# Two heads' value products issued in one block, in the two column halves of the TensorE array

## The chip, the cores and the metric

The kernel runs on one core of one Trainium2 chip. The metric is the device time of one execution in microseconds (us); less is better. Stages of the program are named by the engine that a profile names: PE is TensorE's matmul, PEld its weight load, DVE is VectorE, ACT is ScalarE, POOL is GpSimd, SP is the engine whose queue issues most of the DMAs.

## The reference

One decoder layer on 512 tokens of width 1024: a norm, one wide projection, two attentions side by side, their merge through sigmoid gates, an output projection, and then a mixture of 64 experts of which each token takes two. The two attentions end in a product of probabilities and values; these products are what the change touches.

```python
# forgetting attention, 8 heads of 64, blocks of 128 queries
s = einsum('bqhd,bkhd->bhqk', qb, k) * scale + cb[..., None] - c_k[:, :, None, :]
p = softmax(where(causal, s, -inf))
o_f = einsum('bhqk,bkhd->bqhd', p, v)
# sliding window of 128 with a sink, 8 query heads over 2 key/value heads
s = einsum('bnqhgd,bnkhd->bnhgqk', qb, kw) * HEAD_DIM ** -0.5
p = softmax(concatenate([where(valid, s, -inf), sink]))[..., :-1]
o_s = einsum('bnhgqk,bnkhd->bnqhgd', p, vw)
# experts, per block of tokens
y = (silu(xb @ w1[e]) * (xb @ w3[e])) @ w2[e]
```

Everything is in float32. The weights of the 64 experts are some 400 MB, and every expert is read.

## The kernel before, in words

The program has three stretches. In the first, up to about 62 us, the inputs are normed and transposed and the first projections are made. In the second, up to about 420 us, TensorE makes the remaining projections, both attentions, the gates, the output projection and the routing. In the third the experts run, while SP's queue loads their weights in pieces of 1 MB (tiles `w`) into a ring of 16 buffers, from which they are released by TensorE's matmuls.

The attentions stand in the second stretch, in an order that is written out by hand: a manual schedule on all five engines, so each engine does its work in the order in which the code calls it. `pipeline` runs over steps i. In step i it calls `scores(i)` (TensorE, then a maximum on DVE and an exponential on ACT), `softmax(i - 1)` (DVE scales the probabilities), a piece of the projections by `take`, `probs_t(i - 2)` (TensorE transposes the probabilities; ACT or DVE copies them to `probs_T`), another piece by `take`, and `values(i - 3)`. The projections that `take` feeds in (`acc_vf`, `acc_qf`, `acc_kf`, `acc_g`) are independent of the attention at hand; they are there to keep TensorE occupied.

The sliding-window attention has 16 steps: a block t of 128 queries, a key/value head g, and a pair hp of query heads. Its values are the product of `vs` (64 columns of the key/value head g, the stationary operand) with `probs_T[i]` (256 columns: two heads), over one block of keys for t = 0 and two for the others. The result of g = 0 lies in partitions 0 to 63 of the bank `os_ps`, that of g = 1 in partitions 64 to 127. The forgetting attention has two pipelines of 16 steps: two pairs of heads, j, then four blocks of queries, qb, then the two heads x of the pair. Its values are the product of 64 columns of `vf` with 128 columns of `fprobs_T[i]`, over qb + 1 blocks of keys, into partitions 0 to 63 of `of_ps` for x = 0 and 64 to 127 for x = 1. All of these matmuls use the 128 rows of the array and 64 of its 128 columns; operands in plain float32 are run in two passes, so the profile has two records for each. The other matmuls around them use all 128 columns.

The experts' matmuls use 32 of the 128 columns, four experts in turn (`h`, L1391; `y_ps`, L1410). In the forgetting attention the steps already alternate between the two halves, but each step's values are issued by themselves, a step apart. In the sliding window two steps of the same g come one behind the other.

Lines that matter: L568 and L719 issue the values, L523 and L685 begin the scores, L545 and L698 scale probabilities, L553 and L705 transpose them, L557, L559, L708 and L710 copy them out of PSUM, and L299 to L301 are the three products of a projection in split precision.

Of the kernel before, what the change touches and what calls it, by code (L numbers as in the profile page):

```python
# [20 lines left out]
P = 128  # L21
# [4 lines left out]
HD = 64  # L26
# [71 lines left out]
def kernel(ctx: ExitStack, tc: tile.TileContext, a: dict, out: bass.AP, dbg=None):  # L98
# [3 lines left out]
    v, act, pe, gp = nc.vector, nc.scalar, nc.tensor, nc.gpsimd  # L102
# [13 lines left out]
    def acc_tile(name):  # L116
        return ps.tile([P, 512], F32, tag="acc", name=name, bufs=2)

    def s_tile(name):
        return ps.tile([P, 512], F32, tag="s", name=name, bufs=2)  # L120
# [4 lines left out]
    def o_tile(name):  # L125
        return ps.tile([P, 512], F32, tag="o", name=name, bufs=2)
# [16 lines left out]
    for name in ORDER:  # L143
        kind, i = name.rstrip("0123456789"), int(name[-1]) if name[-1].isdigit() else 0
# [31 lines left out]
    def defer(n, f):  # L176

        deferred.append([n, f])
# [214 lines left out]
    vs = main.tile([P, NT, P], F32, name="vs")  # L393
# [17 lines left out]
    for t in range(NT):  # L411
        s = slice(t * P, (t + 1) * P)
        o = acc_tile(f"acc_kv_{t}")[:, :UNIT]
# [28 lines left out]
    def att_tile(name, dt=F32):  # L442
        return att.tile([P, 512], dt, tag="u", name=name)
# [67 lines left out]
    osT_lo = blk.tile([P, 4, T], F32R, name="osT_lo", tag="ol", bufs=1)  # L511
    probs, probs_T, os_ps = {}, {}, {}

    def swa_scores(i):

        t, g, hp = i // 4, i // 2 % 2, i % 2
        k0, nk = max(t - 1, 0) * P, 256 if t else 128
        s_ps = s_tile(f"ss_ps{i}")
        s3 = s_ps.rearrange("p (h k) -> p h k", h=2)
        for j in range(2):  # L520
            h = 2 * hp + j
            lt = qsT[t, g][:, h * P:(h + 1) * P]
            pe.matmul(s3[:, j], lt, ksT[0][g][:, k0:k0 + 256], start=True, stop=False, skip_group_check=True)  # L523
            pe.matmul(s3[:, j], lt, ksT[1][g][:, k0:k0 + 256], start=False, stop=False, skip_group_check=True)
            pe.matmul(s3[:, j, 0:nk], ident_b, band if t else causal, start=False, stop=True, skip_group_check=True)
        s3 = s3[:, :, 0:nk]
        h0 = 4 * g + 2 * hp
        sm = small[:, i % 4]
        nm, e, sums = (sm[:, 2 * x:2 * x + 2] for x in range(3))
        v.tensor_reduce(nm, s3, axis=AX.X, op=OP.max, negate=True)  # L530
        v.tensor_tensor(nm, nm, neg_sinks[:, h0:h0 + 2], op=OP.min)
        v.tensor_tensor(e, sinks[:, h0:h0 + 2], nm, op=OP.add)
        p_sb = att_tile(f"sp{i}")
        p3 = probs[i] = p_sb.rearrange("p (h k) -> p h k", h=2)[:, :, 0:nk]
        for j in range(2):
            act.activation(p3[:, j], s3[:, j], AF.Exp, bias=nm[:, j:j + 1], accum_out=sums[:, j:j + 1])
        act.activation(e, e, AF.Exp)
# [21 lines left out]
            v.tensor_copy(pT[:, :n], pst[:, :n])  # L559

    def swa_values(i):
        t, g, hp = i // 4, i // 2 % 2, i % 2
        nb = 2 if t else 1
        if i % 4 == 0:
            os_ps[t] = o_tile(f"os_ps{t}")
        o = os_ps[t][g * HD:(g + 1) * HD, hp * 256:hp * 256 + 256]
        for b in range(nb):
            pe.matmul(o, vs[:, max(t - 1, 0) + b, g * HD:(g + 1) * HD], probs_T[i][:, b * 256:b * 256 + 256],  # L568
                      start=b == 0, stop=b == nb - 1, skip_group_check=True)
        if i % 4 == 3:  # L570
            s = slice(t * P, (t + 1) * P)
            o4 = os_ps[t].rearrange("p (r n) -> p r n", r=4)
            act.activation(osT_hi[:, :, s], o4, AF.Copy)
            defer(2, lambda: v.tensor_tensor(osT_lo[:, :, s], o4, osT_hi[:, :, s].bitcast(F32), op=OP.subtract))


    vf = main.tile([P, NT, T], F32, name="vf")
# [64 lines left out]
    fq, fk, fprobs, fsums, fprobs_T, of_ps, ofT = {}, {}, {}, {}, {}, {}, []  # L642
# [30 lines left out]
    def fox_at(i):  # L673

        return i // 16, i // 8 % 2, i // 2 % 4, i % 2
# [34 lines left out]
            v.tensor_copy(pT[:, :nk], pst[:, :nk])  # L710

    def fox_values(i):
        n, j, qb, x = fox_at(i)
        h = 4 * n + 2 * j + x
        qs_ = slice(qb * P, (qb + 1) * P)
        if i % 8 == 0:
            of_ps[n, j] = o_tile(f"of_ps{n}{j}")
        for b in range(qb + 1):
            pe.matmul(of_ps[n, j][x * HD:(x + 1) * HD, qs_], vf[:, b, h * HD:(h + 1) * HD],  # L719
                      fprobs_T[i][:, b * P:(b + 1) * P], start=b == 0, stop=b == qb, skip_group_check=True)  # L720
        if i % 8 == 7:
            hi = blk.tile([P, T], F32R, tag="b", name=f"ofT_hi{n}{j}")
            lo = blk.tile([P, T], F32R, tag="b", name=f"ofT_lo{n}{j}")
            act.activation(hi, of_ps[n, j], AF.Copy)
            defer(2, lambda: v.tensor_tensor(lo, of_ps[n, j], hi.bitcast(F32), op=OP.subtract))
            ofT.append((hi, lo))
# [47 lines left out]
    def swa_extra(i):  # L774
# [5 lines left out]
        if t < NT and j >= 2:  # L780
            queries_T(t, j - 2)

    pipeline(0, 16, swa_scores, swa_softmax, swa_probs_T, swa_values, QUANTA[0], swa_extra)
    take(GAP[1])
    pipeline(0, 16, fox_scores, fox_softmax, fox_probs_T, fox_values, QUANTA[1])
    take(GAP[2])
    last_exp = pipeline(16, 16, fox_scores, fox_softmax, fox_probs_T, fox_values, QUANTA[2])

    fox_done.append(True)
# [127 lines left out]
    for n in range(4):  # L917
# [5 lines left out]
        for m, src_hi, src_lo in (("pf", lambda k: ofT[k][0], lambda k: ofT[k][1]),  # L923
                                  ("ps", lambda k: osT_hi[:, k], lambda k: osT_lo[:, k])):
            hi, lo = halves_of[f"{m}{n}"]
            for j in range(2):
                b = 2 * n + j
                o = acc_tile(f"{m}_ps{b}")
# [4 lines left out]
                g = gates[b if m == "pf" else b + 8]  # L933
# [202 lines left out]
    for t in range(NT):  # L1136
        o = acc_tile(f"out_ps3_{t}")[:, :256]
# [244 lines left out]
    for b in range(N_BATCH):  # L1382
# [3 lines left out]
        for k in range(2):  # L1386
            for o, m in ((h1, "w1"), (h3, "w3")):
                for c in range(4):
                    for e in range(4):
                        s = slice(32 * e, 32 * e + 32)  # L1390
                        pe.matmul(o[s], hsel[:, 4 * k + c, s], wt[b, m, k, e][c], start=(k, c) == (0, 0),  # L1391
                                  stop=(k, c) == (1, 3), skip_group_check=True)
# [13 lines left out]
        for c in range(4):  # L1406
            for k in range(2):
                for e in range(4):
                    s = slice(32 * e, 32 * e + 32)
                    pe.matmul(y_ps[k][s], gT[:, c, s], wt[b, "w2", c // 2, e][c % 2][:, 512 * k:512 * k + 512],  # L1410
                              start=c == 0, stop=c == 3, skip_group_check=True)
# [34 lines left out]
```

## Time and profile before

| what | value |
|---|---|
| median of 3 runs | 1360.95 us (1360.67 to 1361.66) |
| the profiled execution | 1361.19 us |
| its span, first to last instruction | 1359.4 us |
| PE busy | 1215.0 us, 89% of the span |
| DVE, ACT, POOL busy | 469.3, 244.8, 96.8 us |
| records of values, sliding window (L568) | 56 |
| records of values, forgetting attention (L719) | 160 |
| DMA share, 420 us to the end | 0.99, at 410 GB/s |

The profiled execution is 0.24 us from the median, and 1.8 us of it lie outside the span. The page gives busy time per engine, a picture of the span in 40 slices, and the chain of work that ended last, followed back from the last instruction. [...]

### The profile page before, as it was taken

How to read it: one execution, taken by the hardware profiler on the slowest of the kernel's cores; microseconds unless marked ns; L12 is line 12 of the kernel's file. 1: busy time of each engine (PE TensorE's matmuls, PEld its weight loads, DVE VectorE, ACT ScalarE, POOL GpSimd, SP SyncE). 2: the span in 40 equal slices, each digit the busy share in tenths (PEclk: the TensorE clock that was granted, in tenths of full speed). 3: DMA queues.
4: the chain of work that ended last, by engine and by line, in shares of the span. 5: the costliest groups of instructions: out<-in, count | busy, mean ns of one | idle time of the engine just before them, and what ended most of it. 6: DMA issues, size and time to landing. Idle time of an engine off the chain costs nothing.

```text
span 1359.4 us, 17321 instructions
## 1 busy us (share of the span) xinstructions
PE 1215.0 (89%) x6958; PEld 637.7 (47%) x6958; DVE 469.3 (35%) x1173; ACT 244.8 (18%) x560; POOL 96.8 (7%) x135
## 2 busy tenths in 40 slices
PE   7999999999999998989798897979888798979964
PEld 7986677788996433324142333424233232423212
DVE  6776555326446343222123032212213122221203
ACT  4654343433452000000000000000000000000003
POOL 3701000003100000000000000000000000000002
PEclk8999999999999999999899899999899998999988
DMA  5311322238589999999999999999999999999994
GB/s 172 94 52 48 89 49 76 63 93 258 204 301 362 419 421 420 420 420 421 421 420 420 421 421 420 421 421 420 421 420 420 420 421 420 421 420 421 420 413 159
DMA packets 91964, 439.91 MB, mean 324 GB/s; under 512 B 9437, under 2 KB 39177, under 8 KB 43881
## 3 DMA queue, kind: packets, MB, share of 16 engines
q1 hardware_dynamic: 90152, 435.78, 80.1%
q0 software_dynamic: 1728, 2.98, 1.0%
q8 instruction: 56, 0.92, 0.3%
q14 instruction: 28, 0.22, 0.0%
HBM read 434.52 MB, written 2.10 MB: 321 GB/s over the span
## 4 chain that ended last, share of the span: by engine, by line
DMA 65%; PE 29%; DVE 3%; issue 1%; POOL 1%; ACT 1%; SPq 0%; POOLq 0%; ACTq 0%
DMA w<-in_w_dram 65%; PE acc_g L299 2%; PE acc_g L300 2%; PE acc_g L301 2%; PE of_ps L719 2%; PE h L1391 1%; PE os_ps L568 1%; PE acc_wo L301 1%; PE acc_wo L299 1%; PE acc_wo L300 1%; PE acc_kf L299 1%; PE fpT_ps L705 1%; PE acc_qf L299 1%; PE acc_qs L301 1%; PE acc_qs L299 1%
## 5 line engine op out<-in xcount | busy, mean ns | idle before, releaser
L1391 PE MATMUL h<-w,u_hi 128*32 128x512 f32 x2016 | 331.7, 629 | 63.6 <-DMA w<-in_w_dram 63.6
L1410 PE MATMUL y_ps<-w,u_hi 128*32 128x512 f32 x952 | 206.0, 605 | 33.0 <-DMA w<-in_w_dram 29.2
L1391 PEld LDWEIGHTS h<-w,u_hi 128*32 128x32 f32 x2016 | 79.8, 114 | 268.4 <-issue 128.0
L1108 PEld LDWEIGHTS g_ps<-u_hi,xc 128*128 128x128 f32 x1024 | 119.1, 191 | 49.2 <-issue 37.9
L1108 PE MATMUL g_ps<-u_hi,xc 128*128 128x128 f32 x1024 | 130.6, 281 | 1.9 <-DVE u_hi L1062 1.9
L1410 PEld LDWEIGHTS y_ps<-w,u_hi 128*32 128x32 f32 x952 | 49.1, 109 | 177.3 <-issue 87.9
L1214 DVE TENSOR_TENSOR u_lo<-c_ps,u_lo 128x512 f32<-128x512 f32 x84 | 58.1, 691 | 199.1 <-PE c_ps L1208 199.1
L1208 PE MATMUL c_ps<-xb,xb 128*128 128x512 f32 x240 | 116.7, 617 | 1.0 <-DVE u_lo L1211 0.8
L1197 DVE TENSOR_TENSOR u_hi<-h,xb 128x512 f32<-128x512 f32 x16 | 16.5, 1032 | 229.5 <-PE h L1391 229.5
L1196 ACT ACTIVATE xb<-h 128x512 f32<-128x512 f32 x16 | 9.6, 597 | 455.1 <-PE h L1391 455.1
L1189 POOL TENSOR_TENSOR xb<-xb,u_hi 128x512 f32<-128x512 f32 x16 | 20.3, 1271 | 805.9 <-DVE xb L1188 805.9
L1208 PEld LDWEIGHTS c_ps<-xb,xb 128*128 128x128 f32 x240 | 37.8, 188 | 80.0 <-DVE u_lo L1214 36.8
L1058 DVE TENSOR_SCALAR u_hi<-codes,locs,cst 128x128 f32<-128x128 f32 x60 | 20.6, 346 | 155.5 <-PE g_ps L1108 155.3
L1205 ACT ACTIVATE xb<-y_ps 128x512 f32<-128x512 f32 x30 | 17.9, 597 | 224.6 <-PE y_ps L1410 224.6
L299 PE MATMUL acc_g<-hT_hi,hi_g 128*128 128x512 f32 x128 | 54.4, 425 | 0.0
L300 PE MATMUL acc_g<-hT_lo,hi_g 128*128 128x512 f32 x128 | 50.5, 395 | 0.0
L301 PE MATMUL acc_g<-hT_hi,lo_g 128*128 128x512 f32 x128 | 50.5, 394 | 0.0
L1111 DVE TENSOR_TENSOR u_hi<-g_ps,cst 128x512 f32<-128x512 f32 x32 | 21.8, 681 | 59.9 <-PE h L1391 59.5
L1202 ACT ACTIVATE u_hi<-t_ps 128x512 f32<-128x512 f32 x16 | 9.6, 597 | 174.4 <-PE t_ps L1201 174.4
L188 DVE TENSOR_TENSOR lo_g<-raw_g,hi_g 128x1024 fp32r<-128x1024 f32 x16 | 19.6, 1226 | 36.1 <-ACT hi_g L185 36.1
L299 PE MATMUL acc_wo<-hi_wo,mT 128*128 128x256 f32 x96 | 28.6, 298 | 0.0
L301 PE MATMUL acc_wo<-hi_wo,mT 128*128 128x256 f32 x96 | 27.1, 282 | 0.1
(383 smaller groups left out, 1687.9 us busy)
## 6 DMA issues: line engine op xcount, KB each, us to landing
w<-in_w_dram SPq DMA_DIRECT2D x377, 1024.0 KB, 19.8
raw_g<-in_w_in_dram SPq DMA_DIRECT2D x16, 512.0 KB, 3.6
raw_wo<-in_w_out_dram SPq DMA_DIRECT2D x8, 512.0 KB, 4.6
x_sb<-in_x_dram SPq DMA_DIRECT2D x4, 512.0 KB, 6.3
raw_qs<-in_w_in_dram SPq DMA_DIRECT2D x4, 512.0 KB, 6.9
raw_vf<-in_w_in_dram SPq DMA_DIRECT2D x4, 512.0 KB, 4.9
raw_qf<-in_w_in_dram SPq DMA_DIRECT2D x4, 512.0 KB, 3.8
raw_kf<-in_w_in_dram SPq DMA_DIRECT2D x4, 512.0 KB, 3.8
```

What stands on the lines that cost most here:

```text
L299: pe.matmul(o, l_hi, r_hi, start=first, stop=False, skip_group_check=True)
L300: pe.matmul(o, l_hi, r_lo, start=False, stop=False, skip_group_check=True)
L301: pe.matmul(o, l_lo, r_hi, start=False, stop=last, skip_group_check=True)
L719: pe.matmul(of_ps[n, j][x * HD:(x + 1) * HD, qs_], vf[:, b, h * HD:(h + 1) * HD], fprobs_T[i][:, b * P:(b + 1) * P], start=b == 0, stop=b ...
L1058: v.tensor_scalar(sel1[:, t], labels, loc[:, 0, t:t + 1], r, op0=OP.is_equal, op1=OP.mult)
L1108: pe.matmul(g_ps[k][:, c * P:(c + 1) * P], xc[t][:, 4 * k + c], sel1[:, t], start=(t, c) == (0, 0), stop=t == NT - 1, skip_group_check=True)
L1111: v.tensor_tensor(hsel[:, 4 * k:4 * k + 4], g_ps[k].rearrange("p (c n) -> p c n", c=4), g_ffn[:, 4 * k:4 * k + 4, None].to_broadcast([P, 4 ...
L1189: gp.tensor_tensor(wsel, wsel, wtmp, op=OP.add)
L1208: pe.matmul(c_ps, w_t[:, t], ys[k], start=True, stop=True)
L1214: v.tensor_tensor(d, c_ps, d, op=OP.add)
L1391: pe.matmul(o[s], hsel[:, 4 * k + c, s], wt[b, m, k, e][c], start=(k, c) == (0, 0), stop=(k, c) == (1, 3), skip_group_check=True)
L1410: pe.matmul(y_ps[k][s], gT[:, c, s], wt[b, "w2", c // 2, e][c % 2][:, 512 * k:512 * k + 512], start=c == 0, stop=c == 3, skip_group_check= ...
```

## The change

In both attentions the values of a step with an even number are left out, and the step with the odd number behind it issues both: for each block of keys the lower half's matmul, then the upper half's. For that the two steps have to be the two halves of one bank. In the forgetting attention they are already (x = 0 and 1). In the sliding window the order of steps is turned: `swa_at` makes g the fastest index and hp the next, where hp was the fastest before. The bank is opened in the odd step. Nothing else is different: the same matmuls, the same sizes, the same steps of `take`, and on DVE, ACT, POOL and SP the same instructions in the same order.

```diff
+    def swa_at(i):
+
+        return i // 4, i % 2, i // 2 % 2
+
     def swa_scores(i):
 
-        t, g, hp = i // 4, i // 2 % 2, i % 2
+        t, g, hp = swa_at(i)
...
     def swa_values(i):
-        t, g, hp = i // 4, i // 2 % 2, i % 2
+
+        if i % 2 == 0:
+            return
+        t, _, hp = swa_at(i)
         nb = 2 if t else 1
-        if i % 4 == 0:
+        if i % 4 == 1:
             os_ps[t] = o_tile(f"os_ps{t}")
-        o = os_ps[t][g * HD:(g + 1) * HD, hp * 256:hp * 256 + 256]
         for b in range(nb):
-            pe.matmul(o, vs[:, max(t - 1, 0) + b, g * HD:(g + 1) * HD], probs_T[i][:, b * 256:b * 256 + 256],
-                      start=b == 0, stop=b == nb - 1, skip_group_check=True)
+            for g in range(2):
+                o = os_ps[t][g * HD:(g + 1) * HD, hp * 256:hp * 256 + 256]
+                pe.matmul(o, vs[:, max(t - 1, 0) + b, g * HD:(g + 1) * HD],
+                          probs_T[i - 1 + g][:, b * 256:b * 256 + 256],
+                          start=b == 0, stop=b == nb - 1, skip_group_check=True)
...
     def fox_values(i):
-        n, j, qb, x = fox_at(i)
-        h = 4 * n + 2 * j + x
+
+        if i % 2 == 0:
+            return
+        n, j, qb, _ = fox_at(i)
         qs_ = slice(qb * P, (qb + 1) * P)
-        if i % 8 == 0:
+        if i % 8 == 1:
             of_ps[n, j] = o_tile(f"of_ps{n}{j}")
         for b in range(qb + 1):
-            pe.matmul(of_ps[n, j][x * HD:(x + 1) * HD, qs_], vf[:, b, h * HD:(h + 1) * HD],
-                      fprobs_T[i][:, b * P:(b + 1) * P], start=b == 0, stop=b == qb, skip_group_check=True)
+            for x in range(2):
+                h = 4 * n + 2 * j + x
+                pe.matmul(of_ps[n, j][x * HD:(x + 1) * HD, qs_], vf[:, b, h * HD:(h + 1) * HD],
+                          fprobs_T[i - 1 + x][:, b * P:(b + 1) * P], start=b == 0, stop=b == qb,
+                          skip_group_check=True)
```

The order of PE's instructions in the sliding window, before, at the end of the pipeline step that issues the values of step 4 (`spT4`) and begins the scores of step 8 (`ss_ps8`); the last name of each row is the stationary or moving operand, and the size is that of the output:

```order
L299 MATMUL acc_vf1_1_1180<-hi_vf1_1_954,hT_hi_116 128x256
L300 MATMUL acc_vf1_1_1180<-lo_vf1_1_955,hT_hi_116 128x256
L301 MATMUL acc_vf1_1_1180<-hi_vf1_1_954,hT_lo_117 128x256
L568 MATMUL os_ps1_1274<-spT4_1198,vs_127 64x256 x2
L523 MATMUL ss_ps8_1277<-ksT00_444,qsT2_0_1206 128x256
```

The same place after, and one pipeline step further on:

```order
L299 MATMUL acc_vf1_1_1179<-hi_vf1_1_954,hT_hi_116 128x256
L300 MATMUL acc_vf1_1_1179<-lo_vf1_1_955,hT_hi_116 128x256
L301 MATMUL acc_vf1_1_1179<-hi_vf1_1_954,hT_lo_117 128x256
L527 MATMUL ss_ps8_1274<-ksT00_444,qsT2_0_1205 128x256
L528 MATMUL ss_ps8_1274<-ksT10_446,qsT2_0_1205 128x256
```

```order
L299 MATMUL acc_qf0_0_1320<-hT_hi_116,hi_qf0_0_1035 128x512
L300 MATMUL acc_qf0_0_1320<-hT_lo_117,hi_qf0_0_1035 128x512
L301 MATMUL acc_qf0_0_1320<-hT_hi_116,lo_qf0_0_1036 128x512
L576 MATMUL os_ps1_1326<-spT4_1197,vs_127 64x256
L576 MATMUL os_ps1_1326<-spT5_1258,vs_127 64x256
L576 MATMUL os_ps1_1326<-spT4_1197,vs_127 64x256
L576 MATMUL os_ps1_1326<-spT5_1258,vs_127 64x256
L527 MATMUL ss_ps9_1331<-ksT01_445,qsT2_1_1266 128x256
```

The block of step 4 is gone from its place, and its two matmuls stand between those of step 5, a pipeline step later.

PE in the forgetting attention, before, at the values of step 3 (`fpT3`; those of step 2 stand by themselves one pipeline step ahead of this):

```order
L299 MATMUL acc_qf1_0_1880<-hT_hi_116,hi_qf1_0_1717 128x512
L300 MATMUL acc_qf1_0_1880<-hT_lo_117,hi_qf1_0_1717 128x512
L301 MATMUL acc_qf1_0_1880<-hT_hi_116,lo_qf1_0_1718 128x512
L719 MATMUL of_ps00_1829<-fpT3_1878,vf_454 64x128 x2
L685 LDWEIGHTS lq_108
L685 MATMUL sf_ps7_1912<-c3_109,lq_108 128x512
```

And after:

```order
L301 MATMUL acc_qf1_0_1880<-hT_hi_116,lo_qf1_0_1718 128x512
L732 MATMUL of_ps00_1851<-fpT2_1846,vf_454 64x128
L732 MATMUL of_ps00_1851<-fpT3_1878,vf_454 64x128
L732 MATMUL of_ps00_1851<-fpT2_1846,vf_454 64x128
L732 MATMUL of_ps00_1851<-fpT3_1878,vf_454 64x128
L694 LDWEIGHTS lq_108
L694 MATMUL sf_ps7_1912<-c3_109,lq_108 128x512
```

Each pair of value blocks on PE has become one block of twice as many matmuls, in which the two halves alternate.

## Rows read from the trace of the kernel before

**Rows 1.** The page's chain that ended last, shares of the span by engine.

```profile
DMA 65%; PE 29%; DVE 3%; issue 1%; POOL 1%; ACT 1%; SPq 0%; POOLq 0%; ACTq 0%
```

**Rows 2.** That chain in order of time: start, length in us, what.

```profile
442.83 3.69 PE y_ps L1410 x32
...
447.31 16.71 DMA w<-in_w_dram
...
1266.23 19.87 DMA w<-in_w_dram
1286.17 21.37 DMA w<-in_w_dram
```

**Rows 3.** Busy time by stretch: us, engines with (records), PE clock, DMA share, GB/s.

```profile
76.00:142.00 66.00, 66.00 (x380) 48.52 (x379) 44.08 (x124) 34.19 (x99) 3.90 (x7) 1.00 0.23 61
...
153.00:206.00 53.00, 53.00 (x290) 37.69 (x289) 29.37 (x62) 22.45 (x49) 3.29 (x7) 1.00 0.24 63
```

**Rows 4.** Instructions of lines 568 and 719: ns min/median/max, first and last start.

```profile
L568 PE MATMUL os_ps<-spT,vs x56: 379/379/430, 76.3 to 141.1; 128*64 128x256 f32 x56
...
L719 PEld LDWEIGHTS of_ps<-fpT,vf x160: 132/137/137, 153.5 to 258.2; 128*64 128x64 f32 x160
L719 PE MATMUL of_ps<-fpT,vf x160: 272/273/324, 153.5 to 258.3; 128*64 128x128 f32 x160
```

**Rows 5.** PE in order of time, forgetting attention: start, length in us, what.

```profile
149.22 0.40 PE L301 MATMUL acc_g<-hT_hi,lo_g 128*128 128x512 f32 x1
149.46 0.29 PE L685 MATMUL sf_ps<-c,lq 128*128 128x256 bf16 x1
...
171.86 1.09 PE L719 MATMUL of_ps<-fpT,vf 128*64 128x128 f32 x8
172.88 0.28 PE L685 MATMUL sf_ps<-c,lq 128*128 128x256 bf16 x1
...
215.20 0.39 PE L301 MATMUL acc_g<-hT_hi,lo_g 128*128 128x512 f32 x1
215.52 0.43 PE L719 MATMUL of_ps<-fpT,vf 128*64 128x128 f32 x2
215.88 0.34 PE L685 MATMUL sf_ps<-c,lq 128*128 128x384 bf16 x1
```

**Rows 6.** PE in order of time, sliding window.

```profile
76.31 0.65 PE L568 MATMUL os_ps<-spT,vs 128*64 128x256 f32 x2
76.89 0.39 PE L523 MATMUL ss_ps<-ksT,qsT 128*128 128x256 f32 x1
...
120.69 1.08 PE L568 MATMUL os_ps<-spT,vs 128*64 128x256 f32 x4
121.70 0.38 PE L523 MATMUL ss_ps<-ksT,qsT 128*128 128x256 f32 x1
```

**Rows 7.** PE in order of time in the experts: one and three column groups of 32.

```profile
464.74 1.04 PE L1391 MATMUL h<-w,u_hi 128*32 128x512 f32 x2
465.71 0.49 PE L1108 MATMUL g_ps<-u_hi,xc 128*128 128x128 f32 x2
...
505.32 1.06 PE L1391 MATMUL h<-w,u_hi 128*32 128x512 f32 x6
506.31 0.49 PE L1108 MATMUL g_ps<-u_hi,xc 128*128 128x128 f32 x2
```

**Rows 8.** Weight loads of the same three column groups.

```profile
505.31 0.15 PEld L1391 LDWEIGHTS h<-w,u_hi 128*32 128x32 f32 x6
```

**Rows 9.** Where a producer is least ahead of PE: forgetting attention, then sliding window.

```profile
189.50 0.49 DVE L698 TENSOR_SCALAR fp<-fp,sm 128x512 f32<-128x512 f32 x1
...
191.54 0.27 PE L705 MATMUL fpT_ps<-ident,fp 128*128 128x128 f32 x1
...
77.65 0.39 ACT L557 ACTIVATE spT<-spT_ps 128x256 f32<-128x256 f32 x1
...
79.14 0.38 PE L553 MATMUL spT_ps<-ident,sp 128*128 128x128 f32 x2
```

## The prediction

> **What bounds the kernel now.** I read the chain that ended last first. By engine DMA has 65% of it and PE 29% [rows 1]. In order of time it goes over from one to the other once: at 446.5 us PE's first `y_ps` matmuls set buffers free, and from 447.3 us it runs through the weight loads, some 19.9 us each, to the experts' end [rows 2]. So the loads set the length of the third stretch, but their start hangs on PE: whatever PE saves ahead of 442 us moves every later piece forward by the same amount. Nothing in the loads has to be done faster for that; the same bytes are loaded, later pieces are only begun earlier.
>
> [...] Since busy time counts overlapping records, I take costs from distances between starts.
>
> **What one block of values costs.** There are 56 records in the sliding window and 160 in the forgetting attention, two passes for each matmul [rows 4]. In the trace they form 16 and 32 blocks.
>
> Forgetting attention [rows 5]: without values the last projection matmul is followed by the scores after 149.46 - 149.22 = 0.24 us. With a block of two records between them, entry takes 215.52 - 215.20 = 0.32 us and the block 215.88 - 215.52 = 0.36 us to the scores' start: 0.68 us, which is 0.44 us more than without. A block of eight takes 172.88 - 171.86 = 1.02 us, so each record beyond the second costs (1.02 - 0.36) / 6 = 0.11 us. Blocks of two, four, six and eight records therefore cost 0.44, 0.66, 0.88 and 1.10 us, each with a fixed part of 0.44 - 2 x 0.11 = 0.22 us for going into the half-width matmuls and out again.
>
> Sliding window [rows 6]: a block of two takes 76.89 - 76.31 = 0.58 us to the scores, one of four 121.70 - 120.69 = 1.01 us, 0.215 us for each record more. With the same 0.08 us at the entry they cost 0.66 and 1.09 us, fixed part 0.23 us.
>
> **What the change removes.** Of each two blocks of equal size one goes from its place, and its records are put between those of the other. If the two halves of the array work side by side, the block that is left costs what it costs now, and the other block's whole cost is gone.
>
> - sliding window: 2 blocks of two records (t = 0) and 6 of four: 2 x 0.66 + 6 x 1.09 = 7.9 us
> - forgetting attention: 4 pairs of heads, one block of each size: 4 x (0.44 + 0.66 + 0.88 + 1.10) = 12.3 us
> - together 20.2 us
>
> Do halves work side by side? No row of this trace has two 64-column matmuls in different halves next to each other. The nearest are the experts' 32-column groups, which have the same 128 rows, float32 and two passes. One group, two records, takes 465.71 - 464.74 = 0.97 us to the next matmul; three groups, six records, take 506.31 - 505.32 = 0.99 us [rows 7]. The second and third group cost 0.02 us together. So the lower bound of the cost of the added records is nothing, and the upper one that of running in turn, 0.11 or 0.215 us for each record. I take nothing, since the experts' rows differ in the width of the group alone.
>
> The weight loads need a look, because a step of 0.11 us is shorter than one load of 0.137 us [rows 4], and now each step has two. Alone they are already overlapped, at one for each 0.11 us. The six loads of the experts' three groups take 0.15 us in all, though one such load lasts about as long [rows 8]: loads to different columns overlap. I cost the loads at nothing; without that cover the forgetting attention's steps would double and its part of the gain would shrink to the fixed 16 x 0.22 = 3.5 us.
>
> **What the change adds or moves.** No instruction is added on any engine. DVE, ACT, POOL and SP have the same instructions in the same order, so nothing is moved past anything on a queue. Three things follow on PE.
>
> First, the earlier step's probabilities wait one pipeline step longer. Their copy is made earlier than it is needed; the cost is only that a buffer is held longer, and the order of all other work stays.
>
> Second, PE now comes sooner to the transposes and the scores in the steps that have lost their block, and may find a producer late. I looked for the smallest distance between a producer's end and PE's use with a removed block in between. In the forgetting attention DVE has scaled a step's probabilities at 189.99 us and PE transposes them at 191.54 us: 1.55 us ahead, and the removed block of six records there is worth 0.88 us. In the sliding window ACT's copy out of the transposes' bank ends at 78.04 us and PE writes that bank again at 79.14 us: 1.10 us ahead, against a removed block of 0.66 us [rows 9]. So at the tightest places 0.4 to 0.7 us are left, and I put new waits at zero. As a load, DVE's 44.08 us would stand in 66 - 7.9 = 58.1 us, 76%, which is not a bound.
>
> Third, the turned order of the sliding window wants the second g's queries one step sooner. Their transposes and copies are made in the last two steps ahead of the block, a step or more before use, and a step is over 3 us; nothing.
>
> What is late next is nothing new: PE itself, which stays full in these stretches.
>
> **The sum.** The profiled execution took 1361.19 us, of which 1359.4 us are the span; the median is 1360.95 us, and the 0.24 us between them are no matter here. 1360.95 - 20.2 = 1340.7 us, 1.5% less. Five loads of the chain take some 21.4 us in place of 19.9 us, the last of them at 1286 us [rows 2]; with the whole stretch moved by 20 us one more or one less may fall into it, 1.5 us either way.
>
> **The rivals.**
>
> *One pass too many.* The program gives each matmul's two passes one behind the other, lower half first. If starts keep to that order, the upper half's first pass can only begin with the lower half's second, and a merged block takes one step more: 8 x 0.215 + 16 x 0.11 = 3.5 us back, 1344.2 us. Against it: with three groups, six records in such an order would need four steps where one group needs two, and they take 0.99 us against 0.97 us [rows 7]. [...]
>
> *Halves in turn.* If 64-column matmuls, unlike 32-column ones, do not overlap, only the fixed parts go: 8 x 0.23 + 16 x 0.22 = 5.4 us, 1355.6 us. If only their weight loads don't, in the forgetting attention alone: 7.9 + 3.5 = 11.4 us, 1349.6 us. For it: no such pair in the trace. Against it: the experts.
>
> *A producer becomes the limit.* Each of the 24 thinned steps waits for DVE or ACT. With 0.4 us for each, about what is left at the tightest place, 9.6 us come back: 1350.4 us. Against it: both engines have idle time there [rows 3], and the places shown are the tightest.
>
> *Slower: every change of halves is a change of mode.* Into and out of a block of values cost 0.22 us together [rows 5]. If going from the lower to the upper half cost the same and nothing overlapped, a merged block of m matmuls for each head would have 2m - 1 such changes: 20 in the sliding window and 64 in the forgetting attention, 84 x 0.22 = 18.5 us against the 5.4 us of fixed parts: 13.1 us slower, 1374.1 us. It decides from 5.4 / 84 = 0.06 us for each change. Against it: six records over three groups are 0.02 us longer than two over one [rows 7].
>
> That the change does not do what it says would leave 1361 us; the order of PE's instructions shows the pairs, so I give it next to nothing.
>
> **How the numbers follow.** Side by side with no new wait 0.77 (1338.7 to 1342.7 us, by the load that may fall in or out and the rounding of 24 blocks); one pass too many or a share lost 0.07; a late producer 0.05; halves in turn 0.07, split between its two times; slower 0.03; no change 0.01. The range takes the first two whole and the near part of the third and holds some 0.87: 1338 to 1347 us. A measurement of this kernel can tell about 0.2%, 2.7 us, from no change. All cases but the last two end more than that below 1360.95 us: faster 0.95, same 0.02, slower 0.03.
>
> **What would show it.** The same 56 and 160 records, but starts in pairs a few ns apart, and blocks of eight records in the sliding window that take about 1.01 us to the next matmul, as blocks of four do now; in the forgetting attention blocks of 16 in about 1.02 us. Steps without values go from projection to scores in 0.24 us. PE stays without gaps, the first `y_ps` block ends near 426 us, and the weight loads behind it keep their 19.9 us. Starts a whole step apart would show one of the first two rivals, gaps ahead of transposes or scores the third, pieces of 0.2 us between the halves the fourth. The forecast is wrong as a whole if the values shrink as told and the chain's change to DMA still stands at 447 us.

## The result, and the profile after

| what | before | after |
|---|---|---|
| median, us | 1360.99 (4 runs) | 1339.87 (4 runs, 1339.56 to 1340.80) |
| ratio | | 0.9845 (95% interval 0.9828 to 0.9862) |
| span of the profiled execution, us | 1359.4 | 1338.2 |
| PE busy, us | 1215.0 | 1193.7 |
| DVE, ACT, POOL busy, us | 469.3, 244.8, 96.8 | 469.8, 244.3, 96.3 |

The change saves 21.1 us; 20.2 us were forecast, and the time forecast, 1340.7 us, is 0.8 us above the measured one. PE's busy time falls by 21.3 us; that of DVE, ACT and POOL moves by half a microsecond at most. All medians here are of runs in the usual, fast state; one run more of the changed kernel, in a later set, took 3633 us and is in none of them.

The chain that ended last, shares of the span by engine, answers to [rows 1]; then the two lines of values in the grouped view (ns min/median/max, first and last start), which answer to [rows 4]:

```profile
DMA 63%; PE 30%; DVE 3%; issue 1%; ACT 1%; POOL 1%; SPq 0%; POOLq 0%; ACTq 0%
```

```profile
L576 PE MATMUL os_ps<-spT,vs x56: 379/379/430, 79.6 to 132.6; 128*64 128x256 f32 x56
...
L732 PE MATMUL of_ps<-fpT,vf x160: 272/273/324, 147.3 to 237.2; 128*64 128x128 f32 x160
```

The counts of 56 and 160 records and their lengths are those of before. What is new is how closely they stand. PE in order of time (start, length in us, what), first in the sliding window, which answers to [rows 6]: a step that has lost its values, then one that has both heads'.

```profile
76.31 0.28 PE L301 MATMUL acc_vf<-hi_vf,hT_lo 128*128 128x256 f32 x1
76.43 0.28 PE L527 MATMUL ss_ps<-ksT,qsT 128*128 128x256 f32 x1
76.55 0.28 PE L528 MATMUL ss_ps<-ksT,qsT 128*128 128x256 f32 x1
...
94.66 0.40 PE L301 MATMUL acc_qf<-hT_hi,lo_qf 128*128 128x512 f32 x1
94.99 1.08 PE L576 MATMUL os_ps<-spT,vs 128*64 128x256 f32 x8
96.00 0.39 PE L527 MATMUL ss_ps<-ksT,qsT 128*128 128x256 f32 x1
96.23 0.28 PE L528 MATMUL ss_ps<-ksT,qsT 128*128 128x256 f32 x1
```

Eight records take 96.00 - 94.99 = 1.01 us to the scores, what four took before. In the forgetting attention, where [rows 5] had eight records in 1.02 us, blocks of 12 and of 16:

```profile
158.13 0.88 PE L732 MATMUL of_ps<-fpT,vf 128*64 128x128 f32 x12
158.94 0.28 PE L694 MATMUL sf_ps<-c,lq 128*128 128x256 bf16 x1
...
163.00 0.40 PE L301 MATMUL acc_qf<-hT_hi,lo_qf 128*128 128x512 f32 x1
163.33 1.09 PE L732 MATMUL of_ps<-fpT,vf 128*64 128x128 f32 x16
164.36 0.28 PE L694 MATMUL sf_ps<-c,lq 128*128 128x256 bf16 x1
```

Sixteen take 164.36 - 163.33 = 1.03 us. The views group neighbouring records; in the records themselves the starts come in pairs 0.006 to 0.007 us apart, and from the second pair on they follow each other every 0.216 us (256 columns) and 0.109 us (128 columns), the steps of single records before.

The saving keeps to the end. The first block of `y_ps` and one of the last `c_psl`, first after, then before:

```profile
421.60 3.64 PE L1424 MATMUL y_ps<-w,u_hi 128*32 128x512 f32 x32
...
1313.35 3.70 PE L1278 MATMUL c_psl<-xb,xb 128*128 128x512 f32 x8 [0.72 <-ACT xb L1287]
```

```profile
442.76 3.64 PE L1410 MATMUL y_ps<-w,u_hi 128*32 128x512 f32 x32
...
1334.59 3.70 PE L1264 MATMUL c_psl<-xb,xb 128*128 128x512 f32 x8 [0.72 <-ACT xb L1273]
```

The block of `y_ps` stands 442.76 - 421.60 = 21.2 us earlier, and `c_psl` 1334.59 - 1313.35 = 21.2 us. Where it was gained: matmul by matmul, PE is 8.5 us earlier when the forgetting attention begins and 21.1 us when the last values are done. (Ahead of the attentions PE of this execution is 0.23 us late, so the attentions give 21.36 us.) From there to the experts nothing is given back. In the experts' stretch the distance varies from 18.4 to 23.1 us, and at the end it is 21.2 us again.

The chain in order of time around its change to DMA, which answers to [rows 2]:

```profile
421.67 7.00 PE y_ps L1424 x64
...
451.56 2.81 PE h L1405 x24
...
455.67 17.28 DMA w<-in_w_dram
...
473.01 19.85 DMA w<-in_w_dram
```

Here the inferred chain does not go over to the loads right behind `y_ps`, as it did before at 447.31 us, but at 455.67 us, behind a block of `h`, 27 us after that `y_ps` has ended. That place alone would read as a change 8 us later than before; the matmuls of the same stretch stand 21 us earlier. Where the two differ, the starts of the same matmuls in both traces are the measurement, and the chain is a way that was inferred.

### The profile page after: what moved, and what is told of

Read it like the earlier page. It is cut to its first block, busy times and chain, and to the rows that moved or that the text cites. A ratio compares the mean times of both kernels' runs of the same rounds, so it can differ in the third digit from the quotient of the medians.

```text
span 1338.2 us, 17324 instructions
## 1 busy us (share of the span) xinstructions
PE 1193.7 (89%) x6958; PEld 625.8 (47%) x6958; DVE 469.8 (35%) x1173; ACT 244.3 (18%) x560; POOL 96.3 (7%) x135
## 4 chain that ended last, share of the span: by engine, by line
DMA 63%; PE 30%; DVE 3%; issue 1%; ACT 1%; POOL 1%; SPq 0%; POOLq 0%; ACTq 0%
DMA w<-in_w_dram 63%; PE acc_g L299 2%; PE acc_g L300 2%; PE acc_g L301 2%; PE h L1405 2%; PE g_ps L1122 1%; PE c_ps L1222 1%; PE y_ps L1424 1%; PE of_ps L732 1%; PE acc_wo L301 1%; PE acc_wo L299 1%; PE acc_wo L300 1%; PE fpT_ps L714 1%; PE acc_qs L301 1%; PE acc_qs L299 1%
## 5 line engine op out<-in xcount | busy, mean ns | idle before, releaser
L1424 PE MATMUL y_ps<-w,u_hi 128*32 128x512 f32 x952 | 203.3, 598 | 32.6 <-DMA w<-in_w_dram 29.0
L1125 DVE TENSOR_TENSOR u_hi<-g_ps,cst 128x512 f32<-128x512 f32 x32 | 21.8, 682 | 59.9 <-PE h L1405 59.4
```

Source lines behind the costliest of these rows:

```text
L1125: v.tensor_tensor(hsel[:, 4 * k:4 * k + 4], g_ps[k].rearrange("p (c n) -> p c n", c=4), g_ffn[:, 4 * k:4 * k + 4, None].to_broadcast([P, 4 ...
```

## The experiments

**Each attention by itself.** In the first kernel the forgetting attention, in the second the sliding window, is written as it was before.

```diff
     def fox_values(i):
-        if i % 2 == 0:
-            return
-        n, j, qb, _ = fox_at(i)
+        n, j, qb, x = fox_at(i)
+        h = 4 * n + 2 * j + x
...
         for b in range(qb + 1):
-            for x in range(2):
...
+            pe.matmul(of_ps[n, j][x * HD:(x + 1) * HD, qs_], vf[:, b, h * HD:(h + 1) * HD],
+                      fprobs_T[i][:, b * P:(b + 1) * P], start=b == 0, stop=b == qb, skip_group_check=True)
```

> The change in the sliding window alone; the forgetting attention as before. Side by side, with the gain carried whole to the end: the sum for this part was 7.9 us, and the trace of the changed kernel shows PE 8.7 us earlier at the end of this attention, so 8 to 9 us below before, 1352 to 1353 us. If the stretch behind gave part of it back, or both parts had to be there for the gain, it would be within 3 us of before.

> The change in the forgetting attention alone; the sliding window as before. Side by side: the sum for this part was 12.3 us, the trace of the changed kernel shows 12.6 us between the ends of the two attentions, so 12 to 13 us below before, 1348 to 1349 us, and with the sliding window's part the whole 21 us. If the weight loads of two halves did not overlap, this part would be the fixed 3.5 us only, 1357 us.

Measured: the sliding window alone 1352.55 us, ratio 0.9937 (0.9921 to 0.9954), 8.8 us less than the 1361.36 us of before; the forgetting attention alone 1348.41 us, ratio 0.9907 (0.9891 to 0.9924), 12.95 us less. In the first, PE is 8.85 us earlier from the start of the forgetting attention on and 8.79 us at the last `c_psl`; in the second 12.61 us at the end of the attention and 12.77 us at the last `c_psl`. By time the two parts add up to 21.8 us against 21.1 us for the whole, which the intervals don't tell apart; by matched matmuls, less where PE of each execution stands ahead of the attentions, they are 8.7 and 12.7 us against 21.36 us. Neither shows a loss to TensorE's weight loads: in the forgetting attention, where one load takes 0.137 us [rows 4] and a step of two records 0.109 us, 12.95 us were gained and not the 3.5 us expected for loads that do not overlap. By time each is above its sum, by 0.9 and 0.65 us, and the whole by 0.9 us.

**Is it the halves, or only that the blocks are fewer?** Here the sliding window's two steps are again issued in one block, but they are the two head pairs of the same g, whose results lie in the same half; the forgetting attention is as before. So blocks are merged with nothing that could run beside each other. The first version walked the two accumulations of one half in turn.

```diff
         for b in range(nb):
-            for g in range(2):
+            for hp in range(2):
...
-                          probs_T[i - 1 + g][:, b * 256:b * 256 + 256],
+                          probs_T[i - 1 + hp][:, b * 256:b * 256 + 256],
```

> The sliding window alone, with two steps' values in one block too, but of the two steps that write the same half (the order of steps as before, same results). If the gain is from the halves running side by side, only the fixed part of 8 blocks goes: 8 x 0.23 us, and 6 times the 0.10 us by which the second matmul behind a removed block came earlier in the changed kernel, 2.4 us, 1358.5 us, and the block of eight records takes 8 steps of 0.215 us. If the gain is from having half as many blocks, it is like the sliding window's part of the change, 8 to 9 us, 1352 to 1353 us.

Measured: 1358.86 us, ratio 0.9983 (0.9973 to 0.9992). This kernel computes something else than was meant: its result is off by a relative 0.0422, and the reference is off by the same 0.0422 when the first head pair's first block of keys is left out where there are two. The work on PE is the same, but for a clean comparison it was made again with one head pair behind the other:

```diff
-        for b in range(nb):
-            for g in range(2):
+        for hp in range(2):
+            for b in range(nb):
```

> The sliding window alone, two steps' values in one block, of the two steps that write the same half, and each step's accumulation ended before the next one's begins. The same two theories: the fixed part alone, 2.4 us, 1358.5 us, and steps of 0.215 us; or half as many blocks is what counts, 1352.5 us.

Measured: 1358.69 us, ratio 0.9982 (0.9972 to 0.9991), 2.5 us less than before. PE in order of time, a block of eight records:

```profile
95.53 0.40 PE L301 MATMUL acc_qf<-hT_hi,lo_qf 128*128 128x512 f32 x1
95.86 1.94 PE L571 MATMUL os_ps<-spT,vs 128*64 128x256 f32 x8
97.73 0.38 PE L523 MATMUL ss_ps<-ksT,qsT 128*128 128x256 f32 x1
```

Eight records take 1.87 us in one half and 1.01 us over two. Of the sliding window's 8.8 us, 2.5 us therefore come from fewer blocks, and 6.3 us from records that run side by side. This kernel keeps the old order of steps, which the change turns; the blocks alone account for 6 x (1.87 - 1.01) and, for the two blocks of four records (1.01 us here, 0.58 us in the change), 2 x 0.43 us, 6.0 us, so the turned order has no sizeable part in it. This is the second rival of the prediction, in the sliding window: what the change would have given had the halves not overlapped. No such kernel was made for the forgetting attention; there the pairs of starts, 0.006 to 0.007 us apart, show the overlap.

**Does the order within a block matter?** All of the lower half's matmuls, then all of the upper half's, in both attentions.

```diff
-        for b in range(nb):
-            for g in range(2):
+        for g in range(2):
+            for b in range(nb):
...
-        for b in range(qb + 1):
-            for x in range(2):
+        for x in range(2):
+            for b in range(qb + 1):
```

> The whole change, but in each merged block all matmuls of the lower half are issued first and then all of the upper half, instead of in turn. If PE looks past a matmul that waits for its half however many stand there, this is as fast as the change, 1340 us. If it looks past one or two only, the upper half starts late: up to 2m - 1 steps more in a block of m matmuls for each head, 6 x 3 x 0.215 us in the sliding window and 4 x (3 + 5 + 7) x 0.11 us in the other, 10.5 us in all, up to 1350.4 us. The blocks with m = 1 are the same in both orders.

Measured: 1342.84 us, ratio 0.9868 (0.9851 to 0.9884), 3.0 us slower than the change. It lies between the two ends, and the reason is in the larger blocks only. PE in order of time, forgetting attention, blocks of 12 and 16:

```profile
158.26 1.15 PE L732 MATMUL of_ps<-fpT,vf 128*64 128x128 f32 x12
159.34 0.28 PE L694 MATMUL sf_ps<-c,lq 128*128 128x256 bf16 x1
...
163.74 1.58 PE L732 MATMUL of_ps<-fpT,vf 128*64 128x128 f32 x16
165.26 0.28 PE L694 MATMUL sf_ps<-c,lq 128*128 128x256 bf16 x1
```

They take 1.08 and 1.52 us, against 158.94 - 158.13 = 0.81 and 1.03 us in the change: 0.27 and 0.49 us more, four times each, 3.0 us, which is the whole difference. A record does not name its half, but the program's order and the starts tell it. Blocks with up to four records for each half overlap fully: the upper half's first record starts 0.007 to 0.013 us behind the lower's first. With six the first two start alone and the first pair is at 0.269 and 0.275 us, so the upper half starts with the lower's third record; with eight the first four start alone and the pair is at 0.487 and 0.493 us, so it starts with the fifth. So records of one half do start past records of the other that stand ahead of them in the program: at the upper half's first start, three of the lower half's records have not yet started in the blocks of eight (four of each half), in those of 12 (at 0.275 us) and in those of 16 (at 0.493 us). What sets this was not tried.

**Four steps in one block.** If the cost of going into and out of the half-width matmuls is a fixed price for a block, then half as many blocks save it again: 12 blocks in place of 24.

```diff
     def fox_values(i):
-        if i % 2 == 0:
+        if i % 4 < 3:
             return
...
+        for qb in (last_qb - 1, last_qb):
+            qs_ = slice(qb * P, (qb + 1) * P)
             for b in range(qb + 1):
                 for x in range(2):
```

> The change taken a step further: the values of four steps in one block (a whole block of 128 queries of the sliding window; two blocks of queries of the forgetting attention), in turn between the halves as in the change. Blocks: 4 and 8 where the change has 8 and 16. If what is left to win is the fixed part, 4 x 0.23 + 8 x 0.22 us and some five times the 0.10 us by which the second matmul behind a removed block comes earlier, 3.2 us, less than the changed kernel: 1336.7 us. If the producers become the limit, three of four steps being thinned now, waits of up to 1 us ahead of transposes show in the forgetting attention, where the changed kernel has one of 0.26 us, and 1 to 3 us of it are lost: 1338 to 1340 us.

> The changed kernel once more, beside the others of this call: 1340 us.

Measured on one chip: the change 1339.9 us (five runs, 1339.31 to 1340.32), ratio 0.9843 (0.9829 to 0.9856); four steps 1336.17 us (five runs, 1335.88 to 1336.81), ratio 0.9816 (0.9803 to 0.9830). That is 3.7 us less than the change, 3.2 us were expected, and less than either kernel. PE, a block of 16 records in the sliding window and one of 28 in the forgetting attention:

```profile
102.25 1.95 PE L575 MATMUL os_ps<-spT,vs 128*64 128x256 f32 x16
...
161.43 1.75 PE L731 MATMUL of_ps<-fpT,vf 128*64 128x128 f32 x28
163.11 0.28 PE L693 MATMUL sf_ps<-c,lq 128*128 128x256 bf16 x1
```

The 28 records take 1.68 us; the blocks of 12 and 16 that they replace took 0.81 + 1.03 = 1.84 us, and one entry more of 0.33 us, where 0.24 us is the distance without values: 0.16 + 0.09 = 0.25 us for the one block that went.

**The one new wait.** Matched matmul by matmul, PE has one new gap in the changed kernel. In the first forgetting pipeline the transposes of step 14 stand 178.08 - 177.59 = 0.49 us behind the projection, where 0.23 us is the distance without a wait; in the kernel with the forgetting attention alone it is 0.47 us. The changed kernel, PE and then DVE in order of time:

```profile
177.59 0.40 PE L301 MATMUL acc_kf<-hT_hi,lo_kf 128*128 128x512 f32 x1
178.08 0.63 PE L714 MATMUL fpT_ps<-ident,fp 128*128 128x128 f32 x4
```

```profile
172.33 0.68 DVE L660 SCALAR_TENSOR_TENSOR fq<-acc_qf,fq 64x512 fp32r<-64x512 f32 x1 [1.03 <-ACT fq L657]
173.41 1.23 DVE L188 TENSOR_TENSOR lo_g<-raw_g,hi_g 128x1024 fp32r<-128x1024 f32 x1 [0.40 <-ACT hi_g L185]
...
175.35 0.42 DVE L707 TENSOR_SCALAR fp<-fp,sm 128x384 f32<-128x384 f32 x1
...
177.44 0.49 DVE L707 TENSOR_SCALAR fp<-fp,sm 128x512 f32<-128x512 f32 x1
```

DVE ends the scaling at 177.93 us, 0.15 us before PE transposes. Ahead of it on DVE stands a split of 1.23 us that the attention doesn't need yet, and from its start on DVE has no idle time. First this split was given to POOL:

```diff
-        eng = gp if name == "kv_1" else v
+        eng = gp if name in ("kv_1", "g1_0") else v
```

> The changed kernel with one subtraction of 1.23 us (the low part of weight unit g1_0, which stands on DVE ahead of the maxima of steps 14 and 15 of the first pipeline) moved to POOL. If the wait of 0.26 us ahead of the transposes of step 14 is DVE being behind with its queue, it is gone and those transposes follow the projection matmul after 0.23 us; if it is something else (ACT's exponential, PSUM banks), it stays at 0.49 us. The time itself is within 1 us of the changed kernel.

Measured: 1340.34 us, one run. The distance did not shrink but grew. POOL, DVE and PE of this kernel:

```profile
173.67 2.38 POOL L188 TENSOR_TENSOR lo_g<-raw_g,hi_g 128x1024 fp32r<-128x1024 f32 x1 [34.26 <-ACT hi_g L185]
```

```profile
174.04 2.22 DVE L707 TENSOR_SCALAR fp<-fp,sm 128x384 f32<-128x384 f32 x1
```

```profile
177.92 0.39 PE L301 MATMUL acc_kf<-hT_hi,lo_kf 128*128 128x512 f32 x1
178.56 0.63 PE L714 MATMUL fpT_ps<-ident,fp 128*128 128x128 f32 x4 [0.26 <-ACT fp L702]
```

The distance is 0.64 us. While POOL works on the split, DVE's scaling beside it takes 2.22 us, where the same operation takes 0.42 us in the changed kernel. So DVE was late by another way, and the run tells nothing about the cause. (The view names an exponential on ACT as what PE waited for; ACT ends it at 178.57 us, when PE has already started.) The split was then left on DVE and only moved behind the scaling:

```diff
-            defer(wait, lambda: eng.tensor_tensor(lo, r, hi.bitcast(F32), op=OP.subtract))
+            defer(8 if name == "g1_0" else wait, lambda: eng.tensor_tensor(lo, r, hi.bitcast(F32), op=OP.subtract))
```

> The changed kernel with one DVE instruction moved: the split that makes lo_g (line 188, 1.23 us at 173.41 in the changed kernel's trace) comes behind the scaling of step 15 (line 707) instead of ahead of that of step 14. Theory: PE's new wait in the first forgetting pipeline, 0.488 us from the last acc_kf matmul (177.59) to the transposes of step 14 (178.08) where 0.231 us is the distance without a wait, comes from DVE being behind after that split; with 1.23 us of DVE work gone from ahead of it, DVE ends the scaling of step 14 well before PE is there, and the distance is 0.23 us. Rival: the scaling waits for its own inputs (the exponential on ACT) and not for DVE's queue; then the distance stays at 0.45 to 0.50 us. The whole time is 0.26 us lower by the theory and the same by the rival, which is too little to be told by the time; the distance decides.

Measured: 1339.35 us, one run, which tells no difference from the change. DVE and PE:

```profile
176.17 0.49 DVE L707 TENSOR_SCALAR fp<-fp,sm 128x512 f32<-128x512 f32 x1
...
177.63 1.22 DVE L188 TENSOR_TENSOR lo_g<-raw_g,hi_g 128x1024 fp32r<-128x1024 f32 x1
```

```profile
177.30 0.40 PE L301 MATMUL acc_kf<-hT_hi,lo_kf 128*128 128x512 f32 x1
177.53 0.60 PE L714 MATMUL fpT_ps<-ident,fp 128*128 128x128 f32 x4
```

DVE is done 177.53 - 176.66 = 0.87 us ahead, and the distance, 177.53 - 177.30, is 0.23 us again. The wait came from what stood ahead in DVE's queue.

## Why the prediction was right, point by point

- **PE's saving moves all later work.** Right, from end to end. PE is 21.2 us earlier at the first `y_ps` and at the last `c_psl`, though not at every matmul between them. In the kernels with one attention each, 8.85 us at the start of the forgetting attention are 8.79 us at the end, and 12.61 us are 12.77 us. The 1.5 us that one load of 21.4 us more or less might have cost did not fall in.
- **Halves run side by side at no cost.** Right, to 0.007 us for a block, 0.17 us for 24. The experts' 32-column groups [rows 7] were the right neighbour to argue from, and the loads [rows 8] too: with two loads for each step of 0.109 us, 16 records take 1.03 us, where eight with one load for each took 1.02 us [rows 5].
- **The price of a block.** Right: the blocks that went had cost 20.44 us by the distance from the projection to the next matmul; 20.2 us were summed.
- **A term that the sum lacked: 1.3 us.** The cost of a block was read up to the start of the first matmul behind it. The second one is late too: behind a block L528 follows L527 after 96.23 - 96.00 = 0.23 us, and without one after 76.55 - 76.43 = 0.12 us. It shows at 12 of the 24 removed blocks, all 8 in the sliding window and 4 in the forgetting attention whose values are followed by a projection, 0.10 to 0.11 us each. Behind the other blocks stand bf16 matmuls, where no such difference shows: L695 follows L694 after 0.04 us with a block of values ahead and without one.
- **No new wait.** Nearly right, and the step that failed was this one: 0.26 us at one place, which is the very place shown in [rows 9]. There 1.55 us were set against one removed block of 0.88 us. But DVE had not waited for PE's work (a projection, by way of ACT's copy) since 172.33 us, ahead of the split of 1.23 us and more than one step earlier, so two removed blocks counted: 0.66 us of an earlier step, and 0.88 us with its 0.10 us. 1.55 - 0.66 - 0.98 = -0.1 us: nothing is left, and PE starts 0.15 us after DVE's end even so. A slack has to be set against all that PE saves since the producer last had time to spare.
- **The account.** 20.44 - 0.17 + 12 x 0.105 - 0.26 = 21.3 us; the matched matmuls give 21.36 us for the attentions. The lacking 1.3 us and the 0.26 and 0.17 us of the wait and the overlap have opposite signs, so the sum came a little nearer than its terms; that much is luck.

**The rivals.** One pass too many did not come: eight records in 1.01 us leave no room for one more step of 0.216 us. Pairs 0.007 us apart are not one matmul's two records, which stand 0.216 us (256 columns) or 0.109 us (128 columns) or more apart where they have a half to themselves, so the upper half's first record starts ahead of the lower's second, and in the kernel with all of the lower half first it starts ahead of three records of the lower half. Between the halves, then, starts do not keep to the program's order, as this rival had supposed. No run shows the share lost that stands beside it in the chances: sixteen records in pairs take 1.03 us, eight single ones 1.02 us [rows 5]. Halves in turn is ruled out by the same sixteen records, and its price was about right where that kernel was made: 2.5 us for fewer blocks in the sliding window, against 8 x 0.23 = 1.8 us, and 2.6 us with 0.8 us for the second matmul behind each. A late producer came at one place of 24 and for 0.26 us. A change of mode for each change of halves would be a piece of 0.2 us between records; the pairs, 0.006 to 0.007 us apart, leave no room for it.

**The signs told beforehand.** The counts, the blocks of eight and 16, the 0.24 us without values and the end of the first `y_ps` block near 426 us (421.60 + 3.64 = 425.2) came as told. The chain's change to DMA did not: it was to come earlier and comes at 455.67 us. Taken alone it would have spoken against the forecast, which holds all the same; a place in an inferred chain is a weak sign, a matched matmul a strong one.

## What to carry to other kernels

Float32 matmuls on half of the array's columns cost nothing more here when they were paired with as many in the other half (16 records 1.03 us, eight alone 1.02 us). Issue the halves in turn, or at least with no more than four records (two float32 matmuls) of one half ahead of the other's, as in the blocks that overlapped fully, where the other half started 0.007 to 0.013 us behind. Going into and out of a half-width block has a price for each block, 0.22 us here, so gather such matmuls into few blocks where the buffers allow it. When PE gets shorter, set each producer's slack against everything saved since the producer last waited, not against the one block beside it.

## What was not expected of the hardware

- Records of one half started past records of the other half that stood ahead of them in the program, past three in the blocks of eight, 12 and 16. Blocks of 12 and 16 with one half first take 1.08 and 1.52 us, with the halves in turn 0.81 and 1.03 us.
- The cost of leaving a half-width block is not over with the next matmul's start: in the sliding window the second float32 matmul behind it (L528) still comes 0.23 us after the first (L527), where 0.12 us is the distance behind a projection.
- Beside a 128x1024 subtraction on POOL (173.67 to 176.05 us) a DVE scaling took 2.22 us in place of 0.42 us and ended 0.21 us after it. One row shows it; why was not tried.
- Two accumulations in the same partitions of one bank, each begun with its own start flag and then taken in turn, gave a result that is off by a relative 0.0422, as the reference is without the first one's first part. Of the change, which takes two in turn in different halves of the partitions, no such loss was measured.
